# Gated delta-rule layer on one core: products of the identity with itself, added to TensorE between two heads' scans

## The chip, the core and the metric

The kernel runs on one core of a Trainium2 chip. Times are device microseconds of one execution; the metric is the median of the runs. Five engines work side by side, each through its own instructions in order: TensorE (PE, matrix products, with its weight loads PEld overlapped), VectorE (DVE), ScalarE (ACT), GpSimd (POOL) and SyncE (SP, which here issues the transfers). An instruction that waits holds up all that stands behind it on its engine. PE's clock has two levels, 1.2 and 2.4 GHz, and the profile shows the level that was granted.

## The reference, cut to what matters

One layer: a norm and one input projection, a gated delta rule (four heads of width 128, run forward and backward over 2048 positions, with a gated norm at its end) beside windowed attention, one output projection and the residual. What is concerned here is the delta rule. A chunk of 64 positions needs the inverse of a unit triangular matrix, and the chunks of a head follow each other through a state:

```python
    m = jnp.where(strict, jnp.einsum('bhncd,bhnsd->bhncs', k_beta, k) * decay, 0.0)
    t_inv = lax.linalg.triangular_solve(eye + m, jnp.broadcast_to(eye, m.shape),
                                        left_side=True, lower=True, unit_diagonal=True)
    u = jnp.einsum('bhncs,bhnse->bhnce', t_inv, v * beta[..., None])
    w = jnp.einsum('bhncs,bhnsd->bhncd', t_inv, k_beta * jnp.exp(g)[..., None])
...
    def step(state, inp):
        q_i, k_i, u_i, w_i, g_i, a_i = inp
        v_new = u_i - jnp.einsum('bhcd,bhde->bhce', w_i, state)
        o = (jnp.einsum('bhcd,bhde->bhce', q_i * jnp.exp(g_i)[..., None], state)
             + jnp.einsum('bhcs,bhse->bhce', a_i, v_new))
        g_last = g_i[..., -1]
        k_dec = k_i * jnp.exp(g_last[..., None] - g_i)[..., None]
        state = state * jnp.exp(g_last)[..., None, None] + jnp.einsum('bhcd,bhce->bhde', k_dec, v_new)
        return state, o
```

## The kernel before, in words

The first two thirds of the span hold the projections, the convolution, the attention and its half of the output projection, with a partial sum `part` that is made on PE, added on DVE (L561) and stored (L562). Then come the four heads. The kernel uses chunks of 128 positions, so 16 per head and direction (index d, 0 forward, 1 backward).

For a head h the code calls three functions. `pre_front(h)` makes, for four groups of four chunks, what needs no state: it loads `kq` and `vt`, transposes them on PE (`tr`, L641; `trv`, L678), takes the Gram products (`gh`, L661) and multiplies them on DVE by the decay into `ma` (L670). The decay tile `dc` is filled on POOL (L632) and ACT (L669); POOL also takes a power (`nk`, L651). The matrices that have to be inverted go out to memory (`m_d`, L675).

`pre_back(h)` inverts them. The diagonal blocks of 32 are solved on DVE, row after row (tiles `tm` and `X`, L705 and L709, 31 rows each): this is "the solve" below. Its result goes out through a transfer (`x_d`, L710) and comes back by chunk groups (`xc`, L718), is transposed on DVE (`xt`, L719), and copied on POOL into block patterns (`iv` and `ma`, L724, L726, L728, L745). From these, five stages of products on PE (`pi0` to `pi4`, L733, four products of 128x128 each, one group at a time) build the full inverse, with copies on ACT between them (`b`, L742).

`scan(h)` does the 16 steps of both directions in pairs. In a step PE multiplies the state by the keys (`pk`, L773, keys from a transfer `kqc`, L771), DVE subtracts it from the values (`r`, L775), PE applies the inverse (`py`, L782), ACT copies the result (`yk`, `y`), and PE makes the new state and the output (`po`, L784, L791, L800). After step 12 and after the last step a head's output is normalised: squares on ACT (L825), a power on POOL (`sso`, L829), a scaling on ACT (`oacc`, L836), transposes on PE (`tro`, L839), the gate `zt` on DVE.

The heads are called so:

```python
    pre_back(0, H)
    for h in range(3):
        scan(h, H)
        H = pre_front(h + 1)
        pre_back(h + 1, H)
```

This is not the order in which anything runs. After the program is written, a planner (`set_order`) takes all instructions, with their data dependences, the buffers that they share and a cost for each, and lays them out by list scheduling; the order it finds on each engine is then fixed by dependences between neighbours. So work of `pre_front` and of the solve for head h + 1 runs among the steps of scan h, and any instruction that is added can change the order of all others, on every engine and in SP's queue.

In the text below "gap h" is the time between the last step of scan h - 1 (for gap 0: the output of the attention half) and the first step of scan h. "A pair" is the forward and the backward step of one index i.

Of the kernel before, what the change touches and what calls it, by code (L numbers as in the profile page):

```python
# [7 lines left out]
F32 = mybir.dt.float32  # L8
# [7 lines left out]
P = 128  # L16
# [12 lines left out]
def tile_hybrid(ctx, tc, t, out, dbg=None):  # L29
# [28 lines left out]
    with ExitStack() as cb:  # L58
        phase_b(cb, tc, t, ident, consts, hp, mix_dn, mix_sw, kq_d, v_d, zdn_d, zsw_d, dp, out)
# [457 lines left out]
def phase_b(ctx, tc, t, ident, consts, hp, mix_dn, mix_sw, kq_d, v_d, zdn_d, zsw_d, dp, out):  # L517
    nc = tc.nc
    V, A, G, T = nc.vector, nc.scalar, nc.gpsimd, nc.tensor
    dma = nc.sync.dma_start  # L520

    def pool(name, bufs=1, stack=ctx, **kw):
        return stack.enter_context(tc.tile_pool(name=name, bufs=bufs, reuse_waits="tile", **kw))
# [59 lines left out]
    ps_s = pool("ps_s", space=PSUM)  # L583
# [20 lines left out]
    def pre_front(h):  # L604
        H = {}
        ssk = hp.tile([P, NCH], F32, tag="ssk", name=f"ssk{h}", bufs=1)
        nk = hp.tile([P, NCH], F32, tag="nk", name=f"nk{h}", bufs=1)
        bp = hp.tile([P, 2, NCH], F32, tag="bp", name=f"bp{h}")
        ssq = H["ssq"] = hp.tile([P, NCH], F32, tag="ssq", name=f"ssq{h}", bufs=3)
        ck = H["ck"] = hp.tile([P, 2, NCH], F32, tag="ck", name=f"ck{h}", bufs=3)  # L610
        ks = H["ks"] = {}
        vs = H["vs"] = {}
        mp = {}
        ma = H["ma"] = {}
        m_d = dp.tile([2, NCH, 4 * (32 * P + 32)], F32, tag="m_d", name=f"m_d{h}", bufs=2)
# [217 lines left out]
    def post_rows(h, oa, so, c4):  # L833
# [8 lines left out]
        V.scalar_tensor_tensor(zt, tr.rearrange("p c i -> p (c i)"), dnw, zt, ALU.mult, ALU.mult)  # L842
        dma(mix_dn[h, :, c4 * 512 : (c4 + 1) * 512], zt)

    H = pre_front(0)
    with tc.using_default_side("right"):
        with ExitStack() as sw:
# [7 lines left out]
    for h in range(3):  # L855
        scan(h, H)
        H = pre_front(h + 1)
        pre_back(h + 1, H)
    pre_stack.close()
    op = pool("op", 4)  # L860
    ps_c = pool("ps_c", 4, space=PSUM)
# [362 lines left out]
```

## Time and profile before

| | |
|---|---|
| median of 3 runs | 1339.65 us (1338.12 to 1344.18) |
| the profiled execution | 1339.74 us |
| its span in the profile | 1338.0 us, 22553 instructions |
| PE busy | 1258.0 us, 94% of the span, 7162 instructions |
| DVE, ACT, POOL busy | 66%, 53%, 36% |
| PE's share of the chain that ended last | 72% |
| mean granted clock of PE | 0.979 of full speed |

The profiled execution lies 0.09 us over the median, so a row of its trace can be set against the median as it stands. The span is 1.7 us shorter than the time; this remainder lies around the program. The page cuts the span into 40 slices; a digit of its row of the granted clock is in tenths of full speed, where 9 is 90% or more.

### The profile page before, as it was taken

How to read it: one execution, taken by the hardware profiler on the slowest of the kernel's cores; microseconds unless marked ns; L12 is line 12 of the kernel's file. 1: busy time of each engine (PE TensorE's matmuls, PEld its weight loads, DVE VectorE, ACT ScalarE, POOL GpSimd, SP SyncE). 2: the span in 40 equal slices, each digit the busy share in tenths (PEclk: the TensorE clock that was granted, in tenths of full speed). 3: DMA queues.
4: the chain of work that ended last, by engine and by line, in shares of the span. 5: the costliest groups of instructions: out<-in, count | busy, mean ns of one | idle time of the engine just before them, and what ended most of it. 6: DMA issues, size and time to landing. Idle time of an engine off the chain costs nothing.

```text
span 1338.0 us, 22553 instructions
## 1 busy us (share of the span) xinstructions
PE 1258.0 (94%) x7162; PEld 1072.9 (80%) x7162; DVE 885.6 (66%) x2250; ACT 711.3 (53%) x2105; POOL 484.4 (36%) x868
## 2 busy tenths in 40 slices
PE   5999999999999999999999899998979879898998
PEld 4998878788998888888888687778868769788776
DVE  4423387773632399999987899666885877846433
ACT  5422264332433467666667877229868766466310
POOL 1223032100021235755786755228238155170000
PEclk8999999999999999999999999999979989989999
DMA  7442345244443533222334757968567274333776
GB/s 235 135 140 78 104 161 171 73 135 135 148 121 114 163 102 109 72 93 83 96 120 130 249 185 226 291 209 217 144 184 207 84 212 104 94 104 106 233 241 209
DMA packets 219686, 201.16 MB, mean 150 GB/s; under 512 B 48304, under 2 KB 170800, under 8 KB 219568
## 3 DMA queue, kind: packets, MB, share of 16 engines
q1 hardware_dynamic: 219568, 199.73, 48.8%
q8 instruction: 57, 0.93, 0.3%
q14 instruction: 61, 0.50, 0.1%
HBM read 134.59 MB, written 65.08 MB: 149 GB/s over the span
## 4 chain that ended last, share of the span: by engine, by line
PE 72%; DVE 9%; DMA 5%; ACT 5%; POOL 5%; issue 3%; SPq 0%; DVEq 0%; POOLq 0%; ACTq 0%
PE pf_c L186 6%; PE pf_c L187 6%; PE pf_c L188 5%; PE pf_z L186 4%; PE pf_z L187 4%; PE pf_z L188 4%; PE pi L733 4%; PE pt L360 2%; PE pq_q L197 2%; PE pq_q L199 2%; PE pq_q L198 2%; PE pcd L559 2%; PE pcd L560 2%; PE pcd L558 2%; PE pcs L558 2%
## 5 line engine op out<-in xcount | busy, mean ns | idle before, releaser
L237 DVE SCALAR_TENSOR_TENSOR acc<-pf_c,cw,acc 128x512 f32<-128x512 f32 (+1 forms) x192 | 140.0, 745 | 22.7 <-ACT acc L233 20.9
L186 PE MATMUL pf_c<-xhi,wh_c 128*128 128x512 f32 x384 | 149.3, 401 | 1.9 <-DVE acc L237 1.1
L187 PE MATMUL pf_c<-xlo,wh_c 128*128 128x512 f32 x384 | 150.4, 401 | 0.0
L188 PE MATMUL pf_c<-xhi,wl_c 128*128 128x512 f32 x384 | 148.4, 400 | 0.0
L186 PE MATMUL pf_z<-xhi,wh_z 128*128 128x512 f32 x256 | 91.6, 400 | 0.1
L355 POOL TENSOR_SCALAR pr<-pr,st 128x384 f32<-128x384 f32 (+1 forms) x128 | 83.5, 670 | 22.5 <-DVE st L353 19.0
L187 PE MATMUL pf_z<-xlo,wh_z 128*128 128x512 f32 x256 | 91.0, 397 | 0.0
L346 ACT ACTIVATE pr<-pr,st 128x384 f32<-128x384 f32 (+1 forms) x128 | 76.2, 598 | 27.3 <-DVE st L345 26.7
L188 PE MATMUL pf_z<-xhi,wl_z 128*128 128x512 f32 x256 | 90.3, 396 | 0.0
L186 PEld LDWEIGHTS pf_c<-xhi,wh_c 128*128 128x128 f32 x384 | 72.3, 189 | 17.5 <-DVE acc L237 1.9
L188 PEld LDWEIGHTS pf_c<-xhi,wl_c 128*128 128x128 f32 x384 | 72.0, 188 | 14.6
L187 PEld LDWEIGHTS pf_c<-xlo,wh_c 128*128 128x128 f32 x384 | 72.3, 188 | 13.9
L341 DVE CUSTOM_DVE_ANT_0 pr<-s,mask,sink 128x384 f32<-128x384 f32 (+1 forms) x128 | 72.6, 594 | 6.0 <-PE pt L360 2.5
L360 PE MATMUL pt<-ident,pr 128*128 128x128 f32 x368 | 72.8, 276 | 3.3 <-ACT q L323 1.4
L364 ACT ACTIVATE ph<-pt 128x512 fp32r<-128x512 f32 x92 | 53.4, 594 | 40.2 <-PE pt L360 37.3
L365 DVE TENSOR_TENSOR pl<-pt,ph 128x512 fp32r<-128x512 f32 x92 | 62.5, 684 | 9.1 <-ACT ph L364 7.9
L670 DVE SCALAR_TENSOR_TENSOR ma<-gh,bp,dc 128x256 f32<-128x256 f32 x128 | 56.1, 476 | 17.7 <-PE gh L661 10.0
L787 ACT ACTIVATE yk<-py,ck 128x128 f32<-128x128 f32 x120 | 44.0, 367 | 40.4 <-PE py L782 39.1
L360 PEld LDWEIGHTS pt<-ident,pr 128*128 128x128 f32 x368 | 48.6, 141 | 19.2 <-POOL pr L355 4.8
L178 DVE TENSOR_TENSOR wl_c<-ws_c,wh_c 128x512 fp32r<-128x512 f32 x48 | 36.6, 765 | 37.0 <-ACT wh_c L177 24.7
L197 PE MATMUL pq_q<-wh_q,xhi 128*128 128x256 f32 x256 | 58.5, 284 | 0.8 <-ACT sgq L256 0.8
L561 DVE TENSOR_TENSOR xrd<-xrd,pcd 128x512 f32<-128x512 f32 x32 | 20.9, 684 | 55.5 <-PE pcd L560 55.5
(250 smaller groups left out, 3769.9 us busy)
## 6 DMA issues: line engine op xcount, KB each, us to landing
kqc<-kq_d SPq DMA_DIRECT2D x120, 128.0 KB, 2.5
ws_c<-wt SPq DMA_DIRECT2D x48, 256.0 KB, 3.5
xr<-x SPq DMA_DIRECT2D x16, 512.0 KB, 6.0
ws_z<-wt SPq DMA_DIRECT2D x32, 256.0 KB, 3.4
kq<-kq_d SPq DMA_DIRECT2D x16, 512.0 KB, 4.9
xrs<-x SPq DMA_DIRECT2D x32, 256.0 KB, 3.4
part<-xrs SPq DMA_DIRECT2D x32, 256.0 KB, 3.4
m_d<-ma SPq DMA_DIRECT2D x32, 256.0 KB, 4.9
```

Of the source, the lines that this page charges most:

```text
L186: T.matmul(ps, hi[:, k, cs], xhi[b][:, k], start=(k == 0), stop=False)
L187: T.matmul(ps, hi[:, k, cs], xlo[b][:, k], start=False, stop=False)
L188: T.matmul(ps, lo[:, k, cs], xhi[b][:, k], start=False, stop=(k == KC - 1))
L197: T.matmul(ps[:, :n], xh, hi[:, k, :n], start=(k == 0), stop=False)
L237: V.scalar_tensor_tensor(av, ps[:, lo:], cw[:, i, k : k + 1], av, ALU.mult, ALU.add)
L341: V.tensor_tensor_reduce(pr[j][:, :n], ps[:, :n], mask[:, lo * P : hi * P], 1.0, sink[:, hh : hh + 1], ALU.add, ALU.max, accum_out=mx[:, j ...
L346: A.activation(pr[j][:, :n], pr[j][:, :n], AF.Exp, bias=nm[:, j : j + 1], accum_out=den[:, j : j + 1])
L355: G.tensor_scalar(pr[j][:, :n], pr[j][:, :n], den[:, j : j + 1], 1.0, ALU.mult, ALU.mult)
L360: T.transpose(pt[:, j], pr[j][:, (kb - lo) * P : (kb - lo + 1) * P], ident)
L365: V.tensor_tensor(pl, ptf, ph.bitcast(F32), ALU.subtract)
L558: T.matmul(ps, mh[:, k], wh[:, k, ns], start=(k == 0), stop=False)
L670: V.scalar_tensor_tensor(ma[d, c4][:, c], gh[:, k], bp[:, d, cc : cc + 1], gms[d][:, c : c + 1].to_broadcast([P, 2, P]), ALU.mult, ALU.mult,)
```

## The change

After the code of head h + 1 a tile in PSUM is asked for, under the tag `pk` that the scan's first product of a step uses, and PE multiplies the identity by itself into it, 32, 32 and 20 times behind heads 0, 1 and 2. Each product is 128x128 in f32 and runs as two matmuls. Nothing reads the tile. It is written in full each time, and the tag's buffer goes on to the next scan's `pk`.

```diff
--- before.py
+++ after.py
@@ -842,6 +842,11 @@
         V.scalar_tensor_tensor(zt, tr.rearrange("p c i -> p (c i)"), dnw, zt, ALU.mult, ALU.mult)
         dma(mix_dn[h, :, c4 * 512 : (c4 + 1) * 512], zt)
 
+    def warm(h):
+        idle = ps_s.tile([P, P], F32, tag="pk", name=f"warm{h}")
+        for _ in range((32, 32, 20)[h]):
+            T.matmul(idle, ident, ident, start=True, stop=True)
+
     H = pre_front(0)
     with tc.using_default_side("right"):
         with ExitStack() as sw:
@@ -856,6 +861,7 @@
         scan(h, H)
         H = pre_front(h + 1)
         pre_back(h + 1, H)
+        warm(h)
     pre_stack.close()
     op = pool("op", 4)
     ps_c = pool("ps_c", 4, space=PSUM)
```

Where the products land is the planner's doing. The next rows are PE's in gap 1, between the last product of scan 0 (`po_1_15`) and the first inverse product of head 1 (`pi_1_0`), before the change. A name ends in the tile's indices and a running number; "x4" is four in a row.

```order
L800 MATMUL po_1_15_10559<-y_1_15_10562,ma_3_8726 128x128
L661 MATMUL gh_2_1_12147<-kq_2_12094 128x256 x2
L661 MATMUL gh_0_0_12214<-kq_0_12170 128x256 x2
L641 MATMUL tr_3_0_12258<-ident,kq_3_12248 128x128 x4
L661 MATMUL gh_0_1_12225<-kq_0_12170 128x256 x2
L641 MATMUL tr_3_1_12273<-ident,kq_3_12248 128x128 x4
L839 MATMUL tro_0_10591<-ident,oacc_0_9914 128x128 x4
L839 MATMUL tro_3_10604<-ident,oacc_3_9927 128x128
L733 MATMUL pi_1_0_11053<-iv_0_8564,g_0_11039 128x128 x4
```

The same place after the change:

```order
L800 MATMUL po_1_15_10559<-y_1_15_10562,ma_3_8726 128x128
L661 MATMUL gh_0_0_12247<-kq_0_12203 128x256 x2
L848 MATMUL warm_11299<-ident 128x128 x9
L661 MATMUL gh_0_1_12258<-kq_0_12203 128x256 x2
L848 MATMUL warm_11299<-ident 128x128 x16
L661 MATMUL gh_3_0_12323<-kq_3_12281 128x256 x2
L848 MATMUL warm_11299<-ident 128x128
L839 MATMUL tro_0_10591<-ident,oacc_0_9914 128x128 x4
L733 MATMUL pi_1_0_11053<-iv_0_8564,g_0_11039 128x128 x4
```

The products (L848) stand between the last step and the first inverse product, 26 of them in this stretch; the transposes of `kq_3` have moved ahead of it, into the scan. In gap 1 as a whole there are 29 products, 2 more stand beside the last pair ahead of it and 1 behind it. In gap 2 there are 32: ahead of the first inverse product come three `tr`, 7 products, two `gh`, 9 products, two `gh`, 14 products, four `tro`, one `tro`, one product, two `gh` and two `tro`. In gap 3 there are 15, most of them between the stages of the inverse, and 2 ahead of it and 3 behind it.

On DVE the end of the solve has moved against the scan's last pair. These are rows of DVE at the end of scan 0 before the change; `tm_30` and the `X_10932` behind it are the last row of the solve for head 1, `r_0_15` and `r_1_15` are the last pair (before, `r_0_15` stands three rows above this piece):

```order
L705 TENSOR_TENSOR tm_29_11024<-L_10931,X_10932 128x60
L810 SCALAR_TENSOR_TENSOR oacc_3_9927<-po_0_14_10504,egc,oacc_3_9927 128x128
L709 TENSOR_TENSOR X_10932<-X_10932,tm_29_11024 128x2x30
L775 SCALAR_TENSOR_TENSOR r_1_15_10556<-pk_1_15_10554,negc,vs_0_8780 128x128
L705 TENSOR_TENSOR tm_30_11027<-L_10931,X_10932 128x31
L810 SCALAR_TENSOR_TENSOR oacc_0_9914<-po_1_14_10524,egc,oacc_0_9914 128x128
L709 TENSOR_TENSOR X_10932<-X_10932,tm_30_11027 128x31
```

And after it:

```order
L794 SCALAR_TENSOR_TENSOR S_0_14_10512<-S_0_13_10472,egt,po_0_14_10504 128x128
L705 TENSOR_TENSOR tm_30_11027<-L_10931,X_10932 128x31
L794 SCALAR_TENSOR_TENSOR S_1_14_10532<-S_1_13_10492,egt,po_1_14_10524 128x128
L709 TENSOR_TENSOR X_10932<-X_10932,tm_30_11027 128x31
L670 SCALAR_TENSOR_TENSOR ma_2_12060<-gh_2_1_12180,bp_12044,dc_2_0_12131 128x2x128
L775 SCALAR_TENSOR_TENSOR r_0_15_10541<-pk_0_15_10539,negc,vs_3_8846 128x128
L810 SCALAR_TENSOR_TENSOR oacc_3_9927<-po_0_14_10504,egc,oacc_3_9927 128x128
L810 SCALAR_TENSOR_TENSOR oacc_0_9914<-po_1_14_10524,egc,oacc_0_9914 128x128
L811 TENSOR_TENSOR oacc_3_9927<-po_0_14_10504,oacc_3_9927 128x128
L775 SCALAR_TENSOR_TENSOR r_1_15_10556<-pk_1_15_10554,negc,vs_0_8780 128x128
```

Before, the solve's last row stands behind the last pair; after, ahead of it. For head 2, at the end of scan 1, it is the other way round: its last rows stood ahead of `r_0_15` and now stand behind `r_1_15`.

SP's queue has moved in gaps 0 and 3. In gap 0 the rows of before are these, with `part_8535` and `part_8536` the last stores of the partial sum and `xc` the solve's result for head 0:

```order
L562 DMA part_8535<-xrs_0_9456 128x512
L710 DMA x_d_8582<-X_9536 128x1024
L562 DMA part_8535<-xrs_1_9473 128x512
L718 DMA xc_0_0_9635<-x_d_8582 128x4x32
L718 DMA xc_1_3_9639<-x_d_8582 128x4x32
L562 DMA part_8536<-xrs_0_9496 128x512
L718 DMA xc_0_1_9702<-x_d_8582 128x4x32
L562 DMA part_8536<-xrs_1_9513 128x512
```

After the change:

```order
L562 DMA part_8535<-xrs_0_9456 128x512
L562 DMA part_8535<-xrs_1_9473 128x512
L710 DMA x_d_8582<-X_9536 128x1024
L562 DMA part_8536<-xrs_0_9496 128x512
L562 DMA part_8536<-xrs_1_9513 128x512
L718 DMA xc_0_0_9635<-x_d_8582 128x4x32
L718 DMA xc_1_3_9639<-x_d_8582 128x4x32
```

All four stores of `part` now stand ahead of the first `xc`. In gap 3 one load of the next scan's keys, `kqc_0_3`, stood ahead of the four `xc` of head 3; now it stands behind them.

## Rows read from the trace of the kernel before

**Rows 1.** The page: granted clock of PE, 40 slices.
```profile
PEclk8999999999999999999999999999979989989999
```

**Rows 2.** Windows: gap 0, scan 0, gaps 1 to 3; busy us (count) by engine.
```profile
core 0: us, PE busy (x) PEld busy (x) DVE busy (x) ACT busy (x) POOL busy (x), PEclk, DMA share, GB/s
893.50:909.00 15.50, 12.06 (x79) 10.48 (x78) 6.63 (x22) 10.37 (x49) 12.32 (x39) 0.89 0.51 137
910.00:988.00 78.00, 72.70 (x518) 65.33 (x518) 63.37 (x219) 62.35 (x269) 31.98 (x60) 0.96 0.64 172
988.10:1010.30 22.20, 15.98 (x91) 13.67 (x89) 13.00 (x39) 18.09 (x76) 16.41 (x37) 0.77 0.96 256
1087.90:1106.10 18.20, 12.80 (x75) 10.27 (x73) 10.37 (x31) 12.60 (x55) 14.36 (x40) 0.91 0.66 177
1170.20:1181.90 11.70, 9.01 (x49) 8.22 (x47) 1.93 (x10) 7.53 (x33) 9.86 (x30) 0.71 0.34 89
```

**Rows 3.** Windows: the spells of low clock in gaps 1, 2 and 3.
```profile
991.40:1001.40 10.00, 7.13 (x24) 5.80 (x25) 5.91 (x18) 8.50 (x42) 6.26 (x14) 0.50 1.01 256
1097.40:1100.70 3.30, 3.13 (x12) 2.46 (x11) 1.92 (x6) 1.19 (x4) 2.82 (x11) 0.51 0.81 261
1172.40:1179.10 6.70, 5.92 (x28) 5.66 (x27) 0.51 (x2) 3.56 (x17) 5.96 (x17) 0.50 0.26 68
```

**Rows 4.** Windows: two of the four spells of low clock inside scans.
```profile
970.90:977.40 6.50, 5.93 (x25) 4.73 (x24) 5.65 (x20) 4.91 (x19) 2.80 (x2) 0.50 0.14 39
1083.20:1087.00 3.80, 3.80 (x18) 3.50 (x17) 1.54 (x6) 2.15 (x10) 0.01 (x1) 0.55 0.85 244
```

**Rows 5.** Timeline of PE, gap 1: start, length, work, idle before.
```profile
987.85 0.39 PE L800 MATMUL po<-y,ma 128*128 128x128 f32 x2
...
1000.85 1.43 PE L733 MATMUL pi<-iv,g 128*128 128x128 f32 x8
...
1004.41 1.06 PE L733 MATMUL pi<-iv,b 128*128 128x128 f32 x8
1005.31 1.08 PE L733 MATMUL pi<-iv,g 128*128 128x128 f32 x8
...
1008.37 1.16 PE L733 MATMUL pi<-ma,iv 128*128 128x128 f32 x8 [1.32 <-POOL ma L745]
```

**Rows 6.** Timeline of SP's queue, gaps 0, 1 and 3.
```profile
890.80 0.92 SPq L718 DMA_DIRECT2D xc<-x_d  x2
...
986.79 0.33 SPq L710 DMA_DIRECT2D x_d<-X  x1
...
992.73 0.37 SPq L718 DMA_DIRECT2D xc<-x_d  x1
...
1163.72 2.72 SPq L771 DMA_DIRECT2D kqc<-kq_d  x2
1166.55 0.54 SPq L718 DMA_DIRECT2D xc<-x_d  x1
```

**Rows 7.** Timeline of POOL, gap 1: its first and last copies.
```profile
996.55 0.61 POOL L724 COPY iv<-xc 32x128 f32<-32x128 f32 x2 [1.89 <-DMA xc<-x_d]
...
1008.03 0.29 POOL L745 COPY ma<-xt 32x128 f32<-32x128 f32 x1
```

**Rows 8.** Timeline of PE, gaps 2 and 3.
```profile
1087.60 0.46 PE L800 MATMUL po<-y,ma 128*128 128x128 f32 x2
...
1096.44 1.23 PE L733 MATMUL pi<-iv,g 128*128 128x128 f32 x8
...
1169.85 0.49 PE L800 MATMUL po<-y,ma 128*128 128x128 f32 x2
1171.68 1.56 PE L733 MATMUL pi<-iv,g 128*128 128x128 f32 x8 [1.34 <-POOL iv L724]
1174.01 2.05 PE L733 MATMUL pi<-b,iv 128*128 128x128 f32 x8 [0.78 <-ACT b L742]
1175.85 1.91 PE L733 MATMUL pi<-iv,b 128*128 128x128 f32 x8
```

**Rows 9.** Timeline of DVE, gap 0: the last add of part.
```profile
893.86 0.69 DVE L561 TENSOR_TENSOR xrs<-xrs,pcs 128x512 f32<-128x512 f32 x1 [0.44 <-PE pcs L560]
```

## The prediction, made from the kernel before

> **What bounds the kernel now.** I read the page's forty slices first [rows 1]: TensorE (PE) holds full clock nearly everywhere, and the dips all lie behind two thirds of the span, where the four heads' scans are. Up to there PE is busy without a break, so nothing that only reorders it can move that part much. Then I cut the last third into stretches. Call the time between the last step of one scan and the first step of the next a gap: gap 0 stands before scan 0, gaps 1, 2 and 3 before scans 1, 2 and 3. One view gives the busy time of each engine in the gaps [rows 2]: 15.5, 22.2, 18.2 and 11.7 us long, of which PE is busy 12.1, 16.0, 12.8 and 9.0. PE waits there, and its granted clock is 0.77, 0.91 and 0.71 in gaps 1 to 3. A finer cut shows one spell at 1.2 GHz in each [rows 3]: 10.0, 3.3 and 6.7 us, 20.0 in all, in which PE is busy 7.13 + 3.13 + 5.92 = 16.2 us. Each begins after PE has waited, each ends after PE has worked on at the low level. Inside scans 0 to 2 there are four more such spells, of 3.7 to 6.5 us (the longest and the one that ends just ahead of gap 2 are [rows 4]); the change puts hardly anything there.
>
> What ends a gap is a chain over several engines, not PE. In gap 1 PE does the scan's last product at 987.85, and the next head's first inverse product only at 1000.85, 13.0 us on [rows 5]. Between them lie the solve's result going out at 986.79 and coming back as xc, issued at 992.73 [rows 6], and GpSimd (POOL), idle for 1.89 us between a power and the landing of that xc at 996.55, and still copying at 1008.03 [rows 7]; an inverse stage starts at 1008.37, right behind that last copy, and is released by it [rows 5]. So gap 1 is the solve's round trip plus POOL. Gap 3 is mixed: POOL sets the first inverse product (1171.68), but from 1174.01 on three stages of eight matmuls follow each other on PE at low clock [rows 8].
>
> **The change, part by part.** 84 products of 128x128 in f32 are added, two matmuls each. Price: a stage of four such products takes 1005.31 - 1004.41 = 0.90 us at 2.4 GHz [rows 5], 0.225 each; at 1.2 GHz 1175.85 - 1174.01 = 1.84 us [rows 8], 0.46 each. All 84 cost 18.9 us of PE at one level and 38.6 at the other; a transpose has the columns of a product, a product gh twice as many, so I take 0.225 and 0.45 for these. They read only the identity and write a tile that the next scan's pk takes over; they hold no other engine up except through PE's queue. By the order 29, 32 and 15 of them stand in gaps 1, 2 and 3 proper, 8 in the steps beside them: 6.5, 7.2 and 3.4 us. The room for them is PE's idle time, 6.2, 5.4 and 2.7 us [rows 2], plus what the work there gets shorter if the clock stays up, half of the busy time in the spells: 3.6, 1.6 and 3.0 us. 9.8, 7.0 and 5.7 us: gaps 1 and 3 have room, gap 2 is exactly full. If that cover is gone, each product costs its 0.225 us on the path.
>
> But the placing is done by a planner over the whole program, and it moved other rows too; those set most of my sum.
>
> Gap 0 (no product in it). In SP's queue the last two stores of part now stand ahead of the first xc. They wait for adds on VectorE (DVE), of which the last starts at 893.86 and takes 0.69 [rows 9]; the first xc was issued at 890.80 [rows 6]. It goes out some 3.7 us later (893.86 + 0.69 - 890.80); the last transposes of xt stood behind those adds anyway, so I count 2.2 us (bounds 0 and 3.7).
>
> Gap 1. On DVE the solve for head 1 now ends ahead of the scan's last pair of steps, not behind it; a pair takes about 78.0 / 16 = 4.9 us of scan 0 [rows 2], and the end moves by something under half of that, about 2 us. So x_d goes out and xc comes back that much earlier, or up to 3.6 us if xc is also freed of the load of kq that stood ahead of it. POOL then starts behind its power at once: the 1.89 us of idle time go, and the power itself may come earlier. The products queue ahead of the first inverse product: 26 x 0.225 = 5.9 us, three pairs of gh at 0.9 and four transposes at 0.9, in all 9.5 us after the scan, still inside the 13.0. So the products are covered by that wait, as long as they run at full clock. I take -3 us (bounds -4.5 and 0).
>
> Gap 2. The reverse: the solve for head 2 now ends behind the last step, not ahead of it, and ahead of the first inverse product PE's queue holds 31 products (7.0 us), six gh (2.7), seven transposes (1.6) and three of tr (0.7): 12 us. Before, that product started at 1096.44, 8.8 us after the scan's last product at about 1087.6 [rows 8]; so it is some 3 us later. In return the gh pair and the low spell that stood inside the stages after it are gone (0.9 + 1.6 us at most, by [rows 3]). Net +1 us (bounds -1.6 and +4).
>
> Gap 3. SP now issues the four xc ahead of a kqc for which it waited: the pair of kqc held it from 1163.72 to 1166.44, then came xc [rows 6]. Up to 2.7 us earlier; the first inverse product cannot follow all of it, since PE waited only 1.34 us for it behind the end of scan 2 [rows 8]: I count 0.9. Then the clock: three stages at 1.84 instead of 0.90 us are 2.8 us at most; scalar work between them takes part of it back, I count 1.7. -2.6 us (bounds -4 and 0).
>
> Inside the scans the order moves a few us of gh and tr about; PE is not full there and the four spells may come or go. I count 0 (bounds -5 and +5).
>
> Sum: 2.2 - 3 + 1 - 2.6 = -2.4 us on the profiled execution's 1339.74 us, which is the median of the runs (1339.65) to 0.1 us: **1337 us**.
>
> What of a rule for the clock alone? In [rows 3] the spells hold 20.0 us of time but 16.2 us of PE work. The Trainium skill, page "TensorE: Matmul & The Clock Gate", section "Terms", prices a cold spell by its time, as that time x (1 - K/N); with half the clock that would be 10.0 us won here. No run here shows that; the rows give at most half of 16.2.
>
> **The rivals.**
> A, the clock is worth all that PE works at the low level: every spell in the gaps goes and all of its PE time was on the path. 16.2 / 2 = 8.1 us, the moves of the order cancel: 1331.6 us; with the longest spell in the scans gone too (5.93 us busy, so 3.0) 1328.7, with the one before gap 2 as well 1326.8. For it: in gap 3 the low stages do follow each other on the path. Against it: in gap 1, POOL and the round trip end last, whatever PE's clock is. That is what the rule of the Trainium skill just named, "Terms" in "TensorE: Matmul & The Clock Gate", would do here.
> B, slower: the products themselves run at 1.2 GHz ahead of the inverse products. Then the 31 of gap 2 cost 31 x 0.235 = 7.3 us more on the path, and the 26 of gap 1 take 6.1 us more, which uses up the -3 there: -2.4 + 7.3 + 3 = +7.9, 1348 us. It decides where the clock is down when the first product starts: just ahead of gap 2 it was (a spell to 1087.0, [rows 4]). Against it: PE working without waits is what ended every spell in the rows.
> C, the products do not do what they are for: they stand early in a gap, PE waits later in it, the clock falls there all the same. Then gap 3 wins only 0.9 and gap 1 perhaps 1, gaps 0 and 2 lose 2.2 and 1: +1.3, 1341 us.
>
> **How the numbers follow.** 0.44 for my forecast (its own range 1332 to 1342), 0.32 for A, 0.12 for B, 0.12 for C. About 0.5% (6.7 us) is what a measurement of this kernel can tell from no change: faster is below 1333, slower above 1346.4. Faster: most of A (0.27) and the low end of mine (0.05), 0.32. Slower: most of B (0.10) and a little of the rest, from the scans (0.03), 0.13. Same: 0.55. The range goes from 1326 (A with two spells of the scans gone) to 1347 (mine with the upper bounds of gaps 0 to 2 and nothing won in gap 3: 3.7 + 0 + 4 + 0); beyond it lie most of B and the ends of the scans' bounds, some 0.15.
>
> **What would show it.** Granted clock in gaps 1 to 3: near 1.00 if the products do their work, 0.7 to 0.9 as now under C. One product in a row of them: 0.225 us apart, 0.46 under B. Gap 1: xc issued 2 to 4 us after the scan's last product instead of 4.9, the gap some 19 us long instead of 22.2. Gap 2: first inverse product about 12 us after the scan, length 19 us. Gap 3: the middle stages 0.9 us long, length about 9 us. Gap 0: the first xc behind the last of the adds, the gap 2 us longer. I am wrong if the scans' own lengths change by more than the gaps do, since I counted nothing there, or if the time ahead of gap 0 moves by more than a microsecond or two.

## The result, and the profile after

The change makes the kernel slower: 1344.52 us median of 11 runs (1341.23 to 1348.2) against 1341.96 of 11 runs of the kernel before. The measured ratio is 1.0030, 95% interval 1.0016 to 1.0044, so +4.0 us (2.1 to 5.9) of 1340; the two medians alone give 1.0019, or +2.6 us. The forecast was 1337 us, 2.4 under the kernel before. The profiled execution took 1348.2 us, 3.7 over its median; its trace shows where time goes, not how much of it the median has.

Granted clock of PE on the page of the changed kernel, 40 slices ([rows 1] before):

```profile
PEclk9999999999999999999999999899999989999999
```

Windows of the changed kernel: gap 0, scan 0, gap 1, scan 1, gap 2, scan 2, gap 3 (columns as in [rows 2]).

```profile
898.80:917.40 18.60, 13.29 (x82) 11.95 (x82) 7.96 (x24) 11.68 (x54) 12.04 (x38) 0.82 0.57 149
917.40:1003.00 85.60, 75.46 (x532) 66.46 (x531) 66.77 (x225) 66.64 (x289) 37.24 (x65) 0.98 0.64 175
1003.00:1023.80 20.80, 17.90 (x128) 17.09 (x128) 10.90 (x35) 10.71 (x43) 13.62 (x34) 0.92 0.79 215
1023.80:1099.80 76.00, 67.05 (x500) 61.68 (x500) 59.83 (x201) 56.92 (x235) 33.09 (x65) 0.96 0.53 141
1099.80:1118.10 18.30, 17.64 (x142) 16.59 (x140) 10.64 (x32) 14.72 (x64) 13.75 (x35) 1.00 0.80 222
1118.10:1180.60 62.50, 58.56 (x438) 53.54 (x438) 51.02 (x177) 37.15 (x136) 25.41 (x62) 0.97 0.40 105
1180.60:1189.90 9.30, 8.84 (x74) 8.29 (x73) 1.61 (x7) 7.73 (x34) 8.21 (x25) 1.00 0.22 51
```

The products keep the clock up: 0.92, 1.00 and 1.00 in gaps 1 to 3, where it was 0.77, 0.91 and 0.71 [rows 2]. Cut at the same rows of PE, the trace of before has 14.9, 79.5, 22.0, 77.8, 18.0, 64.3 and 11.6 us, and gap 0 begins at 893.8. So gaps 1 and 3 are 1.1 and 2.2 us shorter, gap 2 is as long as before; the loss stands where there is hardly a product: gap 0 is 3.7 us longer, scan 0 6.1, and gap 0 begins 5 us later. Scans 1 and 2 are each 1.8 us shorter.

PE in gap 1, around the start of gap 2 and at the head of gap 3 of the changed kernel ([rows 5, 8] before):

```profile
1002.37 0.61 PE L800 MATMUL po<-y,ma 128*128 128x128 f32 x4
...
1006.57 3.73 PE L848 MATMUL warm<-ident 128*128 128x128 f32 x32
1010.14 1.03 PE L661 MATMUL gh<-kq 128*128 128x256 f32 x4
...
1014.71 1.51 PE L733 MATMUL pi<-iv,g 128*128 128x128 f32 x8 [2.88 <-POOL iv L724]
...
1099.43 0.39 PE L800 MATMUL po<-y,ma 128*128 128x128 f32 x2
...
1110.61 1.06 PE L733 MATMUL pi<-iv,g 128*128 128x128 f32 x8
...
1182.94 1.13 PE L733 MATMUL pi<-b,iv 128*128 128x128 f32 x8
1183.90 1.06 PE L733 MATMUL pi<-iv,b 128*128 128x128 f32 x8
1184.92 1.13 PE L733 MATMUL pi<-iv,g 128*128 128x128 f32 x8
```

16 products take 1010.14 - 1006.57 = 3.57 us, 0.223 each. In gap 3 a stage takes 0.96 us where it took 1.84. But in gap 1 PE still waits 2.88 us for POOL after all its products. Why POOL is late stands in SP's queue and in POOL's rows ([rows 6, 7] before):

```profile
997.15 0.33 SPq L710 DMA_DIRECT2D x_d<-X  x1
1001.28 1.58 SPq L771 DMA_DIRECT2D kqc<-kq_d  x2
1003.02 1.03 SPq L631 DMA_DIRECT2D dc<-gr_d  x2
1004.10 0.50 SPq L675 DMA_DIRECT2D m_d<-ma  x1
1004.71 0.44 SPq L718 DMA_DIRECT2D xc<-x_d  x1
```

```profile
1006.63 1.64 POOL L829 TENSOR_TENSOR sso<-sso,pw 128x8 f32<-128x8 f32 x1 [1.60 <-DVE sso L828]
1011.35 0.63 POOL L724 COPY iv<-xc 32x128 f32<-32x128 f32 x2 [3.08 <-DMA xc<-x_d]
```

The solve's result leaves 5.9 us ahead of the scan's end (1003.0), but a pair of kqc, two dc and an m_d stand ahead of the first xc, which goes out at 1004.71 and lands at 1011.35, after 6.6 us; before it landed after 3.8 (992.73 to 996.55).

### The profile page after: what moved, and what is told of

It is laid out like the page before. It is cut to its first block, busy times and chain, and to the rows that moved or that the text cites. A ratio compares the mean times of both kernels' runs of the same rounds, so it can differ in the third digit from the quotient of the medians.

```text
span 1346.4 us, 22873 instructions
## 1 busy us (share of the span) xinstructions
PE 1271.2 (94%) x7330; PEld 1087.9 (81%) x7330; DVE 887.0 (66%) x2250; ACT 710.8 (53%) x2105; POOL 482.7 (36%) x868
## 4 chain that ended last, share of the span: by engine, by line
PE 68%; DVE 9%; DMA 8%; ACT 7%; POOL 3%; issue 3%; SPq 1%; DVEq 0%; ACTq 0%; POOLq 0%
PE pf_c L186 6%; PE pf_c L187 6%; PE pf_c L188 5%; PE pf_z L186 4%; PE pf_z L187 4%; PE pf_z L188 4%; PE pi L733 3%; PE pt L360 3%; PE pq_q L197 2%; PE pq_q L198 2%; PE pq_q L199 2%; PE pcd L559 2%; PE pcd L560 2%; PE pcd L558 2%; DVE acc L237 1%
## 5 line engine op out<-in xcount | busy, mean ns | idle before, releaser
L186 PEld LDWEIGHTS pf_c<-xhi,wh_c 128*128 128x128 f32 x384 | 72.2, 189 | 17.5 <-DVE acc L237 1.8
L775 DVE SCALAR_TENSOR_TENSOR r<-pk,negc,vs 128x128 f32<-128x128 f32 x120 | 41.6, 346 | 30.3 <-PE pk L773 29.7
```

The source lines that it names most:

```text
L186: T.matmul(ps, hi[:, k, cs], xhi[b][:, k], start=(k == 0), stop=False)
```

## The experiments

Most edits fix the order of all engines in place of the planner's choice, by a table written into the kernel:

```diff
     end, begin, queue = best
+    queue = fixed(insts, eng)
```

The text says what the table holds. One table gives what all traces show: the end of the last product of the attention half's output ("last pcs"), the lengths of the gaps and of scan 0 in us, all read from PE's timeline, and the time's ratio to the kernel before, with 95% interval. The lengths are of one execution each, which lies between 5.5 us under (3 products) and 4.1 us over (81 products) its kernel's median.

| kernel | last pcs | gap 0 | scan 0 | gap 1 | gap 2 | gap 3 | ratio |
|---|---|---|---|---|---|---|---|
| before | 893.8 | 14.9 | 79.5 | 22.0 | 18.0 | 11.6 | 1 |
| the change | 898.8 | 18.6 | 85.6 | 20.9 | 18.3 | 9.4 | 1.0030 (1.0016-1.0044) |
| order alone | 896.6 | 17.6 | 83.6 | 21.4 | 20.1 | 9.4 | 1.0025 (1.0011-1.0039) |
| products alone | 894.4 | 14.3 | 80.1 | 21.3 | 17.0 | 10.6 | 0.9993 (0.9979-1.0008) |
| early order | 898.7 | 17.5 | 81.6 | 20.4 | 17.9 | 11.7 | 1.0041 (1.0027-1.0054) |
| late order | 894.5 | 14.3 | 87.9 | 20.4 | 18.3 | 9.4 | 1.0018 (1.0002-1.0033) |
| front undone | 894.6 | 16.9 | 85.2 | 20.4 | 18.3 | 9.4 | 1.0006 (0.9990-1.0023) |
| mix at scan 1 | 893.3 | 14.6 | 80.3 | 23.0 | 18.3 | 9.4 | 1.0006 (0.9993-1.0019) |
| kqc moved | 893.0 | 14.3 | 81.3 | 22.5 | 17.7 | 10.7 | 0.9997 (0.9979-1.0014) |
| products doubled | 898.2 | 14.6 | 80.1 | 26.1 | 24.2 | 15.0 | 1.0103 (1.0083-1.0124) |
| stores alone | 897.2 | 19.0 | 80.3 | 23.0 | 17.7 | 10.0 | 1.0041 (1.0027-1.0055) |
| chain restored | 928.3 | 17.7 | 83.7 | 19.2 | 18.3 | 9.4 | 1.0243 (1.0224-1.0262) |
| 81 products | 902.0 | 16.3 | 89.1 | 19.0 | 17.4 | 9.8 | 1.0059 (1.0044-1.0074) |
| 3 products | 895.5 | 11.7 | 86.2 | 28.2 | 20.1 | 9.6 | 1.0063 (1.0049-1.0078) |
| stores undone | 897.2 | 16.4 | 85.1 | 20.9 | 18.3 | 9.4 | 1.0013 (0.9997-1.0028) |
| xc first | 896.8 | 14.9 | 79.5 | 21.9 | 17.7 | 11.6 | 1.0004 (0.9989-1.0019) |
| stack | 897.3 | 14.3 | 80.1 | 21.2 | 17.0 | 10.6 | 0.9995 (0.9977-1.0012) |

**Order and products apart.** First the order of the change with its 84 products taken out of every queue ("order alone"), then the order of before with the 84 products put ahead of the rows for which PE waits ("products alone").

> The changed kernel's order on every engine, with the products left out. Theory (the loss comes from the order that the planner gave to the part ahead of gap 1, and the products themselves win a little): slower than before by 4 to 10 us, ratio 1.003 to 1.008, with scan 0 starting some 9 us later and about 6 us longer than before; the clock in gaps 1 to 3 as low as before. Rival (the products themselves cost, the order costs nothing): ratio 0.998 to 1.001.

> The order of the kernel before on every engine, with the 32, 32 and 20 products put by hand ahead of the instructions for which PE waits in gaps 1, 2 and 3. Theory: everything up to the end of scan 0 as before; clock near 1.00 in the gaps; 1 to 5 us faster, ratio 0.996 to 0.999. Rival (the products cost): slower by 2 to 7 us, ratio 1.002 to 1.005, the first inverse products later than before. Rival (the clock is worth all that PE works at the low level): 8 us faster, ratio 0.994.

Order alone: +0.25%, or 3.3 us (1.5 to 5.2). That is less than the 4 to 10 us expected, and by the point values five sixths of the change's loss; scan 0 begins 5.5 us later than before, not 9. Products alone: -0.9 us (-2.8 to +1.1), no change that shows, and just short of the gain expected. Windows of gaps 1 to 3 with the products alone:

```profile
988.80:1010.10 21.30, 19.49 (x153) 17.86 (x152) 12.81 (x38) 18.21 (x76) 16.36 (x37) 1.00 0.90 264
1086.70:1103.70 17.00, 16.53 (x137) 15.96 (x135) 10.47 (x31) 12.57 (x55) 13.47 (x37) 1.00 0.80 227
1168.50:1179.10 10.60, 9.82 (x89) 9.63 (x87) 1.87 (x9) 7.75 (x33) 9.03 (x27) 1.00 0.37 99
```

The clock is full in all three, and they are 0.7, 1.0 and 1.0 us shorter, 2.7 in all: what the clock gives here, less what the products take. So the products do their work and win little; the order loses.

**Which part of the order.** "Early order": the rows of the change up to the last two steps of scan 0, then the order of before, no products. "Late order": the other way round, with products. The cut is the first `pk` of step 14.

> Up to the last steps of scan 0 the order of the changed kernel, from there on the order of the kernel before; no products. Theory: slower than before by 8 to 15 us, ratio 1.006 to 1.011, all of it ahead of gap 1. Rival (the difference ahead of gap 1 was the spread of single executions): ratio 0.999 to 1.001.

> Up to the last steps of scan 0 the order of the kernel before, from there on the order of the changed kernel with its products. Theory: stages up to scan 0 as before, gap 1 to gap 3 as in the changed kernel, 5 to 7 us faster than before, ratio 0.995 to 0.9965. Rival (the products cost): 1.001 to 1.003, as the changed kernel.

The early order alone costs 5.5 us: the sign that the theory gave, but less than its 8 to 15. The late order was expected to win 5 to 7 us and loses 2.4: that half of the theory fell. Its scan 0 is 87.9 us long, 8 over before, with only its last two steps in the new order.

> The changed kernel with one part undone: up to the first step of scan 0 the order of the kernel before, from there on the changed order with its products. Theory (what the change costs is the later solve for head 0, which holds the start of scan 0): scan 0 starts at about 909 us as before, not at 914 to 917; the time is 5 to 8 us under the changed kernel, ratio to before 0.997 to 1.000. Rival (the loss lies in scan 0 and gap 1, where work of the gap was moved into the scan): scan 0 and gap 1 together 105 to 108 us instead of 102, ratio to before 1.002 to 1.004.

> Up to the first step of scan 1 the order of the kernel before, with the 32 products of gap 1 put ahead of PE's waits by hand; from there on the changed order with its products. Theory (the changed order is better from scan 1 on, by 3 to 6 us as the profiles so far show, and worse only ahead of it): 3 to 6 us faster than before, ratio 0.9955 to 0.998. Rival (those stages are shorter only because work was moved out of them into scan 0): no faster than the products in the order of before, ratio 0.9985 to 1.001.

Both put the cut elsewhere: at the first step of scan 0 ("front undone"), and at the first step of scan 1 with the products of gap 1 by hand ("mix at scan 1"). Undoing the front takes the loss down from 1.0030 to 1.0006 by the point values, though the intervals overlap. From scan 1 on, the new order wins nothing in the time, where 3 to 6 us were expected, though its gaps 2 and 3 are as in the change. In "front undone" the rival is seen as well: scan 0 and gap 1 take 105.6 us, not 101.5.

**The rows in SP's queue at gap 0.** The order of before, with these rows alone moved ("stores alone"):

```diff
 L562 DMA part_8535<-xrs_0_9456 128x512
-L710 DMA x_d_8582<-X_9536 128x1024
 L562 DMA part_8535<-xrs_1_9473 128x512
+L710 DMA x_d_8582<-X_9536 128x1024
+L562 DMA part_8536<-xrs_0_9496 128x512
+L562 DMA part_8536<-xrs_1_9513 128x512
 L718 DMA xc_0_0_9635<-x_d_8582 128x4x32
 L718 DMA xc_1_3_9639<-x_d_8582 128x4x32
-L562 DMA part_8536<-xrs_0_9496 128x512
 L718 DMA xc_0_1_9702<-x_d_8582 128x4x32
-L562 DMA part_8536<-xrs_1_9513 128x512
```

> The kernel before with one part of the change alone, no products: in SP's queue at gap 0 the last stores of part stand ahead of the solve's result and the four loads xc, as the change has it. Theory (the first xc has to wait for the last add of part, 894.6): first xc about 4 us later, gap 0 longer by 2 to 4 us, ratio 1.001 to 1.003. Rival (the adds were ahead of xc's transposes anyway): gap 0 within 0.5 us of 14.3 to 14.9, ratio 0.999 to 1.001.

+0.41%: 5.5 us (3.6 to 7.4) for three rows, somewhat over what was expected. The result's way out in SP's queue of the kernel before (the first xc is in [rows 6]); then SP's queue, DVE, and PE's first inverse product in that run:

```profile
888.13 0.33 SPq L710 DMA_DIRECT2D x_d<-X  x1
```

```profile
890.72 2.14 SPq L562 DMA_DIRECT2D part<-xrs  x2
892.90 0.43 SPq L710 DMA_DIRECT2D x_d<-X  x1
896.86 1.45 SPq L562 DMA_DIRECT2D part<-xrs  x2
898.41 2.09 SPq L718 DMA_DIRECT2D xc<-x_d  x4
```

```profile
891.34 0.19 DVE L709 TENSOR_TENSOR X<-X,tm 128x31 f32<-128x31 f32 x1
...
897.28 0.69 DVE L561 TENSOR_TENSOR xrs<-xrs,pcs 128x512 f32<-128x512 f32 x1 [0.44 <-PE pcs L560]
```

```profile
903.09 1.22 PE L733 MATMUL pi<-iv,g 128*128 128x128 f32 x4 [5.85 <-POOL iv L724]
```

The solve ends at 891.53, but its result waits 1.4 us behind a store; and the first xc goes out 5.5 us after the result (898.41 - 892.90), where it was 2.7 us before (890.80 against 888.13). 1.4 + 2.8 = 4.2 us, and gap 0 is 4.1 longer. Then the same nine rows undone in the changed kernel, and turned further round in the kernel before, with both last stores behind all four xc:

> The changed kernel with its products and its order, but with the nine rows of SP's queue at gap 0 (four stores of part, the solve's result out, four loads xc) in the sequence of the kernel before. Theory (those rows carry most of the loss, as the run with the stores alone was 5.7 us slower): gap 0 back from 18.6 to 14 to 15 us, time 3 to 6 us under the changed kernel, ratio to before 0.998 to 1.001. Rival (the rest of the order ahead of scan 0 costs as much by itself, and in this order the stores are off the chain): gap 0 at 17 to 19 us, ratio 1.002 to 1.004.

> The kernel before with the opposite move alone, no products: the last two stores of part behind the four loads xc, not between them. Theory (these loads are the chain that starts POOL's copies and with them scan 0): the third and fourth xc 2 to 3 us earlier, gap 0 shorter by 0.5 to 2 us, ratio 0.998 to 1.000. Rival (POOL's copies, busy without a break in gap 0, set its end): gap 0 at 14.3 to 14.9 us, ratio 0.999 to 1.001.

Undone in the change, 1.0013: 2.3 us less than the change by the point values, though the intervals overlap. Gap 0 is 16.4 us, between rival and theory: other rows in it cost as well. Storing later still wins nothing (gap 0 14.9): POOL works there without a break from 897.8 us to the gap's end at 911.7, as the rival said.

**Restoring the chain alone** failed as an experiment. Everything on which the solve for head 0 depends kept the place of before, all else that of the change.

> The changed kernel with its products, but everything that the solve of head 0 depends on, up to its result's transfer, takes the place in the order that it had before; attention, the output of the attention half and all else keep the places of the change. Theory (the start of scan 0 is late because the planner put rows of attention ahead of that chain): first row of the solve at about 855 to 856 us as before, not 859 to 861, scan 0 from 909 to 912 us instead of 914 to 917, ratio to before 0.999 to 1.002. Rival (the output of the attention half is stretched by its own transfers and adds, whatever the solve does): scan 0 starts at 914 to 917 us, ratio 1.002 to 1.004.

The mixture of two orders stretched the attention part itself (last pcs 928.3), and the first row of the solve came at 888, not 855. It tells nothing of the question.

**What a product costs without cover, and the row of kqc.** Twice the products at the same places in the order of before; and, without products, `kqc_0_3` of scan 3 behind the four xc.

```diff
-        for _ in range((32, 32, 20)[h]):
+        for _ in range((64, 64, 40)[h]):
```

> The order of the kernel before with twice the products, 64, 64 and 40, at the same places as the 84 of the run with products alone. That run left PE idle for 1.8, 0.5 and 0.8 us in gaps 1 to 3. Theory (a product beyond the idle time costs its 0.225 us on the path): 18.9 us more of PE less those 3.1, so gaps longer by 12 to 16 us in all against that run, ratio to before 1.008 to 1.011. Rival (PE is not what ends a gap): gaps longer by less than 6 us, ratio under 1.004.

> The kernel before with one row moved: in SP's queue the load kqc_0_3 of scan 3 behind the four loads xc of head 3, as the change has it; no products. Theory (gap 3 got shorter by that row, not by the clock): gap 3 about 9.4 to 10 us instead of 11.6, with the clock back near 1.00 without any product; time 1 to 2 us less, ratio 0.998 to 1.000. Rival (the products shorten gap 3): gap 3 stays at 11 to 12 us, clock 0.7.

Doubled: the three gaps take 26.1 + 24.2 + 15.0 = 65.3 us instead of 48.9, 16.4 more, and the time is +1.03%. Just over the 12 to 16 expected: beyond PE's idle time each product is on the path. The kqc row is not settled: gap 3 was 10.7 at a clock of 0.84, but "stores alone", where nothing near gap 3 was moved, shows it shorter and at full clock:

```profile
1177.50:1187.50 10.00, 6.11 (x47) 5.52 (x47) 1.96 (x9) 7.47 (x33) 8.49 (x26) 1.00 0.35 96
```

**Nearly the same change, planned anew.** 31, 31 and 19 products, and a single one each, with the planner's own order.

> The change with 31, 31 and 19 products instead of 32, 32 and 20; the planner lays out the whole program anew. Three products are 0.7 us of PE. Theory (the time is set by the order that the planner happens to find, not by the products): another order ahead of scan 0 and another time, 3 to 8 us off that of the change, more likely under it, ratio to before 0.997 to 1.001. Rival (the products set the time): within 1 us of the change, ratio 1.002 to 1.004.

> The change with a single product behind each of heads 0 to 2. Three products are 0.7 us of PE and keep no clock up: clock in gaps 1 to 3 about 0.75 to 0.9. Theory (the order alone sets the time): a time that differs from before by 1 to 6 us either way, with scan 0 starting at another time than before. Rival (the products set the time): ratio 0.9995 to 1.0005.

+0.59% and +0.63%. By the point values, three products fewer cost 3.9 us against the change, and three products in all, 0.7 us of PE, cost 8.4 us against none. The theory had the direction open and its range missed, but the point stands: the planner's order sets the time, at a size several times that of the products.

**The pieces together.** Order of before, products by hand, kqc row, stores behind xc.

> The order of the kernel before with three things together: the 84 products placed by hand, kqc_0_3 of scan 3 behind the four xc of head 3, and the last two stores of part behind the first four xc. Theory (the pieces add up): gaps 1 and 2 as with the products alone (21.3 and 17.0), gap 3 about 9.4, gap 0 at most 14.3; 2 to 5 us faster than before, ratio 0.996 to 0.9985. Rival (what a gap gives is taken back in the scans): ratio 0.999 to 1.001.

0.9995 (0.9977 to 1.0012): the 2 to 5 us expected did not come, and no version here beats the kernel before.

## Why the prediction was wrong

The kernel moved the other way than I forecast. That its time still lies inside the stated range is luck: errors of several us in different stages partly cancelled.

**The clock and the price of a product: right.** 0.223 us against 0.225; clock 0.92, 1.00 and 1.00; the low stages of gap 3 gone. The first inverse product of gap 2 came 1110.61 - 1099.43 = 11.2 us after the scan's last product, where I had said 12, and gap 2 changed by +0.3 for +1.

**Gap 3: right size, owner open.** -2.2 for -2.6, but with the order alone, without one product, gap 3 has the same 9.4 us and a clock of 1.00. So the new order has this length without the products, at least in that execution. My 1.7 us for the clock there fits 11.6 against 10.0 in the order of before at 0.71 and at 1.00.

**Gap 1: mis-sized.** -3 was forecast, -1.1 came. The step "x_d goes out and xc comes back that much earlier" failed in its second half. x_d left 5.9 us ahead of the scan's end instead of 1.5, and xc went out 2.3 us after the scan's last product, as forecast; but other rows of SP's queue stood ahead of it and it landed after 6.6 us, not 3.8. That is 8.4 us behind the scan's end, where it was 8.3.

**Scan 0, counted at nothing: wrong.** The step that failed is "inside the scans the order moves a few us of gh and tr about; PE is not full there", counted as 0; ACT's rows were not named. Scan 0 is 6.1 us longer, 4.1 with the order alone. A row that moves into the scan stands in its engine's queue ahead of a step of the scan, whether or not the engine has idle time elsewhere. ACT, PE and DVE at the end of scan 0 in the changed kernel:

```profile
993.40 2.44 ACT L669 ACTIVATE dc<-dc,ngc 128x128 f32<-128x128 f32 x8
995.74 0.35 ACT L787 ACTIVATE yk<-py,ck 128x128 f32<-128x128 f32 x1
...
996.14 0.49 PE L791 MATMUL po<-yk,ks 128*128 128x128 f32 x2 [0.79 <-ACT yk L787]
...
998.88 1.08 PE L641 MATMUL tr<-ident,kq 128*128 128x128 f32 x4 [1.26 <-DMA kq<-kq_d]
999.76 0.63 PE L773 MATMUL pk<-S,kqc 128*128 128x128 f32 x2
```

```profile
986.73 0.34 DVE L775 SCALAR_TENSOR_TENSOR r<-pk,negc,vs 128x128 f32<-128x128 f32 x1
...
996.67 0.35 DVE L794 SCALAR_TENSOR_TENSOR S<-S,egt,po 128x128 f32<-128x128 f32 x1 [1.37 <-PE po L791]
996.94 0.18 DVE L709 TENSOR_TENSOR X<-X,tm 128x31 f32<-128x31 f32 x1
997.04 0.48 DVE L670 SCALAR_TENSOR_TENSOR ma<-gh,bp,dc 128x256 f32<-128x256 f32 x1
997.43 0.34 DVE L775 SCALAR_TENSOR_TENSOR r<-pk,negc,vs 128x128 f32<-128x128 f32 x1
...
1000.43 0.35 DVE L775 SCALAR_TENSOR_TENSOR r<-pk,negc,vs 128x128 f32<-128x128 f32 x1 [1.95 <-PE pk L773]
```

and before, the 25th of the 30 rows r, the last two, and the same fills of dc:

```profile
974.74 0.35 DVE L775 SCALAR_TENSOR_TENSOR r<-pk,negc,vs 128x128 f32<-128x128 f32 x1
...
984.52 0.35 DVE L775 SCALAR_TENSOR_TENSOR r<-pk,negc,vs 128x128 f32<-128x128 f32 x1
...
985.95 0.35 DVE L775 SCALAR_TENSOR_TENSOR r<-pk,negc,vs 128x128 f32<-128x128 f32 x1
```

```profile
992.65 2.43 ACT L669 ACTIVATE dc<-dc,ngc 128x128 f32<-128x128 f32 x8
```

The scan's last copy yk stands on ACT behind eight fills of the next head's dc, 2.44 us that lay in gap 1 before; PE waits 0.79 us for it and DVE 1.37 us for PE. Then the last pk stands on PE behind four transposes of kq that wait 1.26 us for their load, and the last two rows r are 3.0 us apart instead of 1.4. The solve's last row takes 0.18 us there and is no cause that this trace shows. The fills stand ahead of that yk in all four kernels that have the change's order from scan 0 to gap 1 (the change, order alone, front undone, stores undone); the wait for kq is 0.46, 0.24 us and nothing in the other three. In all, ACT does 289 instructions in the scan where, cut at the same rows, it did 272, and 43 in the gap where it did 76: work of gap 1 was drawn into the scan.

Scan 0 and gap 1 together are 105.0 to 106.5 us in these four kernels, and 101.3 to 103.8 in the kernel before and in those that keep its order there (the doubled products aside). With the early order, whose last steps are those of before, it is 102.0. That these rows are the cause is read from the traces; no run moved them alone. Nor are they all of it: the 25th of the scan's 30 rows r, well ahead of them, starts 69.3 us into the scan (986.73) where it was 66.0 (974.74), in the early order too, and what costs that stays open.

**Gap 0: the term was mis-sized and its second half missed.** I counted 2.2 us (up to 3.7) for xc behind the last adds. Gap 0 of the change is 3.7 longer, and the rows alone measure 4.1 in gap 0 and 5.5 in the time: the store also held x_d, and the transposes that I took for cover did not cover it, because POOL's first copies need xc itself.

**Ahead of gap 0: "nothing that only reorders it can move that part much" is not borne out, nor settled.** Last pcs lies at 896.6 to 898.8 in the four kernels with the change's order there, and at 893.0 to 898.2 in ten with that of before: 2.5 us in the mean, inside the spread of single executions. The early order costs 5.5 us in time; gap 0 accounts for 2.6 of these.

**The rivals.** A (the clock is worth all low PE work, 8.1 us) is not borne out: with full clock in every gap the time moves by -0.9 (-2.8 to +1.1), the gaps by 2.7. That is less what the products take: PE is idle there for only 1.8, 0.5 and 0.8 us of gaps 1 to 3, and gap 3 in the order of before is 10.6 us with the products and 10.0 without, both at full clock. What the clock alone is worth in gaps 1 and 2 no run shows; in gap 3 it is 1.6 us (11.6 against 10.0, single executions). The Trainium skill's rule for a cold spell ("TensorE: Matmul & The Clock Gate", "Terms") would give 10.0 us for the three spells, an estimate, and 3.4 for the 6.7 us of gap 3; the traces do not agree with it there. B is out: the products of gap 1 ran at 0.223, and gap 2 had full clock. C was right in its sign and wrong in its reason: the clock rose in all three gaps.

The sum failed by the order, not by the products: of the four gap terms only gaps 2 and 3 were near, and the scans, counted at nothing, changed by +6.1, -1.8 and -1.8 us.

## What to carry to other kernels

Where a planner lays out the whole program, an edit that is free by itself can re-roll the order everywhere: time the new order without the edit, and the edit in the old order, before judging it. Filling PE's idle time kept the clock up here but took 2.7 us off gaps with 20 us of low clock; work out such a gain from the engine that ends each wait, not from the cold time. Work that moves out of a gap is not gone: look for it in the queues of the scan beside it. In an in-order queue of transfers, look for a store that waits for late work ahead of a load that starts the next chain: three such rows cost more here than 84 products.

## What the runs showed of the hardware

In gap 3 the granted clock is 1.00 in all ten profiles that have 81 products or more. In the seven with at most three it is 0.71 three times, 0.84 once and 1.00 three times. Without products it falls or holds in one and the same order of the rows around it: 0.71 in the kernel before, in the early order and with xc first (11.6, 11.7 and 11.6 us), 1.00 in "stores alone" (10.0 us).

Much of the spread of single executions arises ahead of the scans: with the same order there, last pcs ranges over 5.2 us, while gap 2 without products repeats to 0.3 us (17.7 to 18.0).
